# Loading every second weight chunk with a casting DMA of GpSimd, and making its low part by a negation and an adding DMA

## The chip, the cores and the metric

The kernel runs on one core of one Trainium2 chip. The metric is the time of one execution on the device, in microseconds (us), taken as the median of several runs. The core has five engines, which run apart from each other and wait on semaphores: TensorE (PE, matmuls), VectorE (DVE), ScalarE (ACT), GpSimd (POOL) and SyncE (SP). SP and POOL issue DMAs, and all of these run on the core's 16 DMA engines.

## The reference, cut to what matters

A trunk of two layers works on 256 tokens of 1024 features, in float32. Each layer is a feed-forward block, a token mixer and a second feed-forward block, and each of these is wrapped in norms:

```python
x = x + 0.5 * rms_norm(swiglu(rms_norm(x, pre1), w_gate_up1, w_down1), post1)
x = x + rms_norm(hybrid_mixer(rms_norm(x, pre_m), w_in, ..., w_o), post_m)
x = x + 0.5 * rms_norm(swiglu(rms_norm(x, pre2), w_gate_up2, w_down2), post2)
# swiglu(h): g, u = split(h @ w_gate_up); (silu(g) * u) @ w_down,  D_FF = 2816
# hybrid_mixer: z = h @ w_in (6144 columns), a gated width-3 convolution, pooling over
# 2, 4, 8, 16 tokens with small group products, two gated projections, then @ w_o
```

The weights are 216 MB in float32. Every weight is read once.

## The kernel before, in words

**Precision.** A matmul in the type float32r uses only the upper part of a float32's mantissa. To get a float32 product the kernel splits every operand into a high part (`hi`, the value rounded to float32r) and a low part (`lo`, value minus high part). A product is then high times high, high times low, and low times high, summed in PSUM.

**Stream of weights.** The weights are cut into 206 chunks of 128 partitions by 2048 float32 (1.05 MB), listed in the order of use in `stream`. A stage is one sublayer: 33 chunks of a feed-forward block (22 of gate and up by turns, 11 of the down product), or 37 of a mixer. The stages begin at chunks 0, 33, 70, 103, 136 and 173. `issue` (L105) starts a chunk: two DMAs of SP, of 512 KB each, into buffers named `raw` (five halves in all), then four parts for each chunk: ACT casts a half of `raw` into `hi`, DVE subtracts it from `raw` into `lo`, and the same for the second half. The parts are put in the list `parts` and taken from it one by one by `part()`, which stands at chosen places between the other work of ACT and DVE. PE, ACT and DVE keep the order of the program (`InOrder`), while the order on POOL and SP is that of a scheduler.

**Depth.** There are five `hi` and five `lo` buffers (`LOOK + 1`). When the product of chunk i is written, chunk i+4 is started, into the buffers that chunk i-1 leaves. A `raw` buffer is free as soon as DVE has subtracted, so that a DMA into it can run ahead of that.

**Products.** `feat_product` (features on partitions) makes 32 matmuls of one chunk; for each eighth of the chunk a matmul with `hi` is followed by one with `lo`, so both parts are needed at once. `out_product` ends a stage: its last three chunks (`TAIL`) are first used for tokens 0 to 127 (block 0), half of the columns after the other, and then for block 1, the first of the three chunks ahead of the other two. While block 1 is on PE, the norms of block 0 run on ACT, DVE and POOL, and its normed rows are turned by PE and cast into `xt` by ACT (`turn`). `fill` then begins the next stage with its first three chunks, block 0 ahead of block 1, so that block 1's norms are covered in turn. POOL computes the power -0.5 of each norm (tile `r`, L207).

**Evictions.** `add_up` copies one half of a product out of PSUM by ACT and adds the other by DVE. PSUM has eight banks, and a product of features holds two.

Of the kernel before, what the change touches and what calls it, by code (L numbers as in the profile page):

```python
# [10 lines left out]
F32 = mybir.dt.float32  # L11
# [3 lines left out]
ALU = mybir.AluOpType  # L15

P = 128
T = 256
D = 1024
# [16 lines left out]

# Columns of the per-feature parameters: gate bias, conv taps, pool bias, pool scale.
F_BG, F_CW, F_PB, F_PS, F_N = 0, 16, 40, 48, 56


class InOrder:
    """An engine whose instructions are kept in the order of the program."""

# [9 lines left out]
def trunk(ctx: ExitStack, tc: tile.TileContext, x, gains, feat, wgu1, wd1, win, wco, wpg, wpo, wo, wgu2, wd2, out):  # L53
    nc = tc.nc
# [17 lines left out]

# [1 line left out]
    xs = [const.tile([P, D], F32, name=f"x{b}") for b in range(NB)]  # L74
# [12 lines left out]

# [1 line left out]
    stream = []  # L89
# [15 lines left out]
    ready = {}  # L105
    state = {"issued": 0, "used": 0}

    def issue(now=True):
        """Loads and splits the next chunk, or leaves the parts of the split for part()."""
        i = state["issued"]  # L110
        state["issued"] = i + 1
        name, l, c = stream[i]
        hi = whi.tile([P, CHUNK], F32R, name="hi")
        lo = wlo.tile([P, CHUNK], F32R, name="lo")
        h = CHUNK // 2
        for s in range(2):
            sl = slice(s * h, (s + 1) * h)
            raw = raws.tile([P, h], F32, name="raw")
            nc.sync.dma_start(raw, src[name][l, c, :, sl])
            parts.append(lambda sl=sl, raw=raw: act.copy(hi[:, sl], raw))  # L120
            parts.append(
                lambda sl=sl, raw=raw: dve.tensor_tensor(lo[:, sl], raw, hi[:, sl].bitcast(F32), op=ALU.subtract)
            )
        ready[i] = (hi, lo)
        if now:
            part(4)
# [8 lines left out]
    def chunk(name, held=0):  # L135
        """The next chunk; held: how many of the chunks before it are still to be read."""
        i = state["used"]
        assert stream[i][0] == name, (stream[i], name)
        state["used"] = i + 1
        top_up(held + 1)  # L140
        if state["issued"] == i + 1:
            part(len(parts))
        return ready.pop(i)

    def top_up(held):
        """Loads and splits ahead, into the buffers that are not held; held chunks are still to be
        read. The last split is left to part()."""
        part(len(parts))
        while state["issued"] < min(state["used"] + LOOK + 1 - held, len(stream)):
            part(len(parts))  # L150
            issue(False)

# [1 line left out]
    def split(dst, src_ap, between=0):  # L154
        """dst = (high, low) views; src in PSUM or SBUF, float32."""
        hi, lo = dst
        act.copy(hi, src_ap)
        part(between)
        dve.tensor_tensor(lo, src_ap, hi.bitcast(F32), op=ALU.subtract)

    def feat_product(name, acts_hl):
        """W^T @ act for the two 128-column tiles of a chunk, features on partitions. In each of the
        two banks: the high weights with the high and with the low part of act side by side, and the
        low weights with the high part on top of the first."""
        ps = [bank(), bank()]
        whi_, wlo_ = (t.rearrange("p (k c) -> p k c", c=CC) for t in chunk(name))
        for i in range(2):
            cs = slice(i * P, (i + 1) * P)
            for k in range(KT):
                both, ah, _ = acts_hl[k]  # L170
                pe.matmul(ps[i], whi_[:, k, cs], both, start=(k == 0), stop=False)
                pe.matmul(ps[i][:, :T], wlo_[:, k, cs], ah, start=False, stop=(k == KT - 1))
        return ps

    def add_up(ps, tag, out=None):
        """The two halves of a feature product, added: [128, 2, 256]."""
        t = tmp.tile([P, 2, T], F32, name=tag)
        out = t if out is None else out
        for i in range(2):
            act.copy(t[:, i, :], ps[i][:, T:])  # L180
        part()
        for i in range(2):
            dve.tensor_tensor(out[:, i, :], ps[i][:, :T], t[:, i, :], op=ALU.add)
        return out

    def token_product(o, w, acts_hl, b, ks):
        """o[128 tokens of block b, 256] = act^T @ W chunk."""
        whi_, wlo_ = (t.rearrange("p (k c) -> p k c", c=CC) for t in w)
        for n, (i, w) in enumerate(((0, whi_), (1, whi_), (0, wlo_))):
            for k in ks:  # L190
                a = acts_hl[k][1 + i][:, b, :]
                pe.matmul(o, a, w[:, k, :], start=(n == 0 and k == 0), stop=(n == 2 and k == KT - 1))

# [1 line left out]
    def load_gain(l, which):  # L195
# [4 lines left out]
    def rstd(parts, scale):  # L200
        """(scale * (sum of parts / D + eps)) ** -0.5"""
        v0 = small.tile([P, 1], F32, name="v0")
        dve.tensor_scalar(v0, parts[0], scale / D, scale * EPS, op0=ALU.mult, op1=ALU.add)
        v1 = small.tile([P, 1], F32, name="v1")
        dve.tensor_scalar(v1, parts[1], scale / D, v0, op0=ALU.mult, op1=ALU.add)
        r = small.tile([P, 1], F32, name="r")
        nc.gpsimd.tensor_tensor(r, v1, mhalf, op=ALU.pow)  # L207
        return r
# [7 lines left out]
    def post(b, banks, gain, scale):  # L216
        """x[b] += rms(h) * gain / sqrt(scale)"""
        u = wide.tile([P, D], F32, name="u")
# [15 lines left out]
    def pre(b, gain, r=None):  # L234
        """rms(x[b]) * gain"""
        if r is None:
# [8 lines left out]
    def turn(b, s):  # L245
        """Half of the next sublayer's input of block b, features on partitions, split."""
        xn, xt = state["xn"][b], state["next"][0]
# [11 lines left out]
    def act_slot(dtype=F32):  # L259
        """[128, 2, 512] float32, or twice that in bfloat16"""  # L260
        return acts.tile([P, 2, 512], dtype, name="act", tag="act")

    def split_pair(src_ap):
        """Two feature tiles [128, 2, 256] -> (high and low side by side, high, low) of each"""
        t = act_slot(F32R).rearrange("p i (h t) -> p i h t", h=2)
        split((t[:, :, 0, :], t[:, :, 1, :]), src_ap, 1)
        return [(t[:, i], t[:, i, 0, :], t[:, i, 1, :]) for i in range(2)]

# [1 line left out]
    def out_product(name, nchunk, acts_hl, on_block):  # L270
# [40 lines left out]
    def fill(name, n, turns, acts_hl, take):  # L311
        """n chunks' products, tokens on partitions. Block 0 goes ahead, and after turns[s] halves of
        a product the s-th half of block 1's input is turned. take(b, f, ps) reads the columns of
        one or two chunks, the f-th the last."""
        ws = [chunk(name, LOOK) for _ in range(n)]
# [16 lines left out]

# [1 line left out]
    def turn_back(tok):  # L334
        """[128 tokens, 2, 256 features] of both blocks, as [128 features, 2, 256 tokens] in PSUM."""
        pt = bank()
# [5 lines left out]
    def ffn(l, gu, dn, acts_hl, on_block, nfill, turns, gains_):  # L342
        # The first nfill chunks: gate and up of a pair by turns, and a last gate.
        slot = act_slot()
# [31 lines left out]
    def mixer(l, acts_hl, on_block, nfill, turns, gains_):  # L376
# [3 lines left out]

        # Gates of the conv branch, the first of block 0 ahead of block 1.
        slots = [act_slot() for _ in range(2)]
# [22 lines left out]

        # Gated short convolution.
        ys = []
# [17 lines left out]

        # Pooling over trailing windows.
        ds_ = []
# [21 lines left out]

        # Gates of the pool branch.  # L450
        gp = gates()
# [30 lines left out]

# [1 line left out]
    plan = []  # L484
    for l in range(DEPTH):
        plan += [("ffn", l, "gu1", "d1", 0, 1, 4.0), ("mix", l, None, None, 2, 3, 1.0), ("ffn", l, "gu2", "d2", 4, 5, 4.0)]

    # The tensor engine's clock rises only after some time of work.
    idle = act_slot(BF16)[:, 0, :]
# [54 lines left out]
def _cols(w):  # L544
    """[L, 1024, N] -> [L, N / 256, 128, 8 * 256]: chunks of 256 columns, partitions first."""
    l, k, n = w.shape
# [4 lines left out]
def _rows(w):  # L551
    """[L, K, 1024] -> [L, K / 256, 128, 2 * 1024]: chunks of two row tiles, partitions first."""
    l, k, n = w.shape
# [4 lines left out]
def _gate_up(w):  # L558
    """Chunks of gate columns and of up columns by turns."""
    c = _cols(w)  # L560
# [35 lines left out]
```

## Time and profile before

| What | Value |
|---|---|
| median of 3 runs | 1187.08 us (1185.7 to 1188.16) |
| span of the profiled execution, first to last instruction | 1184.7 us |
| median less this span | 2.4 us |
| PE, DVE, ACT busy | 1169.6, 804.2, 639.1 us |
| granted TensorE clock, mean | 0.995 of full speed |
| DMA | 224.48 MB on SP's queue, 190 GB/s over the span |

The profiled execution's own time is not given apart from its span; the span is one execution's, and the three runs lie 1.0 to 3.5 us above it. A busy share counts the time in which an engine has an instruction in work; the busy share of DMA is that of the packets on the 16 DMA engines.

### The profile page before, as it was taken

The page shows a single profiled execution, that of the slowest core. Times are in us where ns is not written, and L with a number is a line of the kernel's source. Part 1 is how long each engine was busy: PE and PEld are TensorE (multiplying, and loading weights), DVE is VectorE, ACT ScalarE, POOL GpSimd, SP SyncE. Part 2 cuts the span into 40 slices and gives each one's busy share as a digit, 9 for nine tenths or more (in the row PEclk, how much of TensorE's full clock was granted, in tenths as well). Part 3 has the DMA queues.
Part 4 walks back from the last instruction along what each step waited for, and adds up shares of the span by engine and source line. Part 5 has one row for each costly group of instructions (what it writes and reads, how often), then busy time and mean ns, then how long its engine had stood idle before and what let it go on. Part 6 is the DMA issues. An engine that isn't in the chain of part 4 may idle for free.

```text
span 1184.7 us, 17127 instructions
## 1 busy us (share of the span) xinstructions
PE 1169.6 (99%) x6625; PEld 1023.1 (86%) x6625; DVE 804.2 (68%) x1092; ACT 639.1 (54%) x997; POOL 17.2 (1%) x75
## 2 busy tenths in 40 slices
PE   7999999999999999999999999999999999999997
PEld 6888888988888898888898888898888888988886
DVE  5776745677987776665476666466789786766742
ACT  5755634655564565554365555356556565655630
POOL 0000000000000000000000000000000000000000
PEclk8999999999999999999999999999999999999999
DMA  7765663655566465667456566536565554756540
GB/s 267 265 188 192 194 228 132 222 184 179 171 202 209 163 230 183 196 190 231 161 193 192 185 195 230 189 128 215 182 204 185 198 181 141 243 184 194 190 167 36
DMA packets 62577, 225.57 MB, mean 190 GB/s; under 512 B 7200, under 2 KB 7200, under 8 KB 62496
## 3 DMA queue, kind: packets, MB, share of 16 engines
q1 hardware_dynamic: 62496, 224.48, 57.5%
q8 instruction: 52, 0.85, 0.3%
q14 instruction: 29, 0.24, 0.1%
HBM read 223.40 MB, written 1.05 MB: 189 GB/s over the span
## 4 chain that ended last, share of the span: by engine, by line
PE 96%; ACT 1%; DVE 1%; DMA 1%; POOL 0%; issue 0%; SPq 0%; DVEq 0%; POOLq 0%; ACTq 0%
PE ps L49 96%; ACT junk L49 1%; DMA x<-in_x 1%; POOL r L207 0%; DVE x L49 0%; DVE xn L49 0%; DVE v L49 0%; DVE lo L49 0%; ACT xt L49 0%; ACT hi L49 0%; SPq L78 0%; DVEq L592 0%; POOLq L592 0%; SPq L197 0%; ACTq L49 0%
## 5 line engine op out<-in xcount | busy, mean ns | idle before, releaser
L49 PE MATMUL ps<-xt,hi 128*128 128x512 f32 x1920 | 667.3, 392 | 0.0
L49 DVE TENSOR_TENSOR lo<-raw,hi 128x1024 fp32r<-128x1024 f32 x412 | 495.0, 1221 | 134.5 <-ACT hi L49 133.5
L49 PE MATMUL ps<-xt,lo 128*128 128x256 f32 x1920 | 537.7, 280 | 0.0
L49 ACT CAST hi<-raw 128x1024 fp32r<-128x1024 f32 x412 | 424.9, 1050 | 103.1 <-PE ps L49 89.1
L49 PEld LDWEIGHTS ps<-xt,hi 128*128 128x128 f32 x1920 | 359.2, 187 | 78.7
L49 PEld LDWEIGHTS ps<-xt,lo 128*128 128x128 f32 x1920 | 362.9, 189 | 0.1
L49 PE MATMUL ps<-hi,act 128*128 128x512 f32 x832 | 260.0, 390 | 0.0
L49 PEld LDWEIGHTS ps<-hi,act 128*128 128x128 f32 x832 | 156.2, 188 | 32.3
L49 PE MATMUL ps<-lo,act 128*128 128x512 f32 x416 | 161.9, 389 | 0.0
L49 ACT COPY h<-ps 128x256 f32<-128x256 f32 x150 | 54.5, 374 | 142.9 <-PE ps L49 141.6
L49 DVE TENSOR_TENSOR h<-ps,h 128x256 f32<-128x256 f32 x150 | 61.6, 420 | 91.7 <-ACT h L49 91.7
L49 ACT COPY sil<-ps 128x256 f32<-128x256 f32 (+1 forms) x126 | 46.7, 374 | 103.5 <-PE ps L49 103.5
L49 PE MATMUL ps<-act,hi 128*128 128x512 f32 (+1 forms) x320 | 102.0, 375 | 0.0
L49 PEld LDWEIGHTS ps<-lo,act 128*128 128x128 f32 x416 | 78.1, 188 | 15.7
L49 PE MATMUL ps<-act,lo 128*128 128x256 f32 x288 | 81.0, 281 | 0.0
L49 DVE TENSOR_TENSOR sil<-ps,sil 128x256 f32<-128x256 f32 x106 | 43.7, 420 | 49.1 <-ACT sil L49 49.1
L49 PE MATMUL ps<-hi,xt 128*128 128x256 f32 x512 | 74.4, 289 | 0.8 <-ACT hi L49 0.8
L49 ACT CAST act<-h 128x512 fp32r<-128x512 f32 x65 | 40.4, 621 | 60.9 <-DVE h L49 60.9
L49 PEld LDWEIGHTS ps<-hi,xt 128*128 128x128 f32 x512 | 67.7, 196 | 1.6 <-ACT hi L49 1.2
L49 PEld LDWEIGHTS ps<-act,hi 128*128 128x128 f32 x320 | 58.1, 189 | 12.0
L49 PEld LDWEIGHTS ps<-act,lo 128*128 128x128 f32 x288 | 54.5, 189 | 0.0
L49 DVE TENSOR_TENSOR act<-h,act 128x512 fp32r<-128x512 f32 (+1 forms) x73 | 50.1, 686 | 6.0 <-ACT act L49 5.7
(57 smaller groups left out, 450.2 us busy)
## 6 DMA issues: line engine op xcount, KB each, us to landing
raw<-in_wgu SPq DMA_DIRECT2D x176, 512.0 KB, 4.6
raw<-in_win SPq DMA_DIRECT2D x96, 512.0 KB, 4.7
raw<-in_wd SPq DMA_DIRECT2D x88, 512.0 KB, 4.6
raw<-in_wco SPq DMA_DIRECT2D x16, 512.0 KB, 5.2
raw<-in_wpo SPq DMA_DIRECT2D x16, 512.0 KB, 4.2
raw<-in_wo SPq DMA_DIRECT2D x16, 512.0 KB, 4.4
gain<-in_gains SPq DMA_DIRECT2D x12, 512.0 KB, 4.6
raw<-in_wpg SPq DMA_DIRECT2D x4, 512.0 KB, 4.2
```

What stands on the lines that cost most here:

```text
L49: return lambda *a, **kw: self.tc.keep_in_program_order(f(*a, **kw))
```

## The change: what it does

From chunk 5 on, every odd chunk (5, 7, ... 205: 101 of the 206) takes another way. One DMA of POOL of 1.05 MB reads the weights from HBM and casts them into `hi`. ACT writes `lo = -hi`, in two halves. A second DMA of POOL reads the same weights again and adds them onto `lo`, which leaves value minus high part. These chunks use no `raw` buffer and nothing of DVE. The list of parts has for such a chunk the two negations, the issue of the adding DMA, and an empty part, so that the places of `part()` stay in step. The even chunks, and chunks 1 and 3, stay as they were. The comments were taken out, too, which moves the line numbers.

```diff
         hi = whi.tile([P, CHUNK], F32R, name="hi")
         lo = wlo.tile([P, CHUNK], F32R, name="lo")
         h = CHUNK // 2
+        ready[i] = (hi, lo)
+        if i > 3 and i % 2:
+
+            w = src[name][l, c]
+            nc.gpsimd.dma_start(hi, w)
+            for s in range(2):
+                sl = slice(s * h, (s + 1) * h)
+                parts.append(lambda sl=sl: act.mul(lo[:, sl], hi[:, sl].bitcast(F32), -1.0))
+            parts.append(lambda: nc.gpsimd.dma_start(lo, w, accum_op=ALU.add))
+            parts.append(lambda: None)
+            if now:
+                part(4)
+            return
         for s in range(2):
...
-        ready[i] = (hi, lo)
         if now:
             part(4)
```

On ACT, in the first gate and up stage, before the change. Here `ps_716` and `ps_717` are the banks of an up product, `hi_721` is chunk 13, four further on than that product's, and `sil_812` takes the next gate product:

```order
L49 COPY h_759<-ps_716 128x256 [waits PE_49,Activation_49]
L49 COPY h_759<-ps_717 128x256 [waits PE_49]
L49 CAST hi_721<-raw_723 128x1024 [waits DMAHW2_49]
L49 CAST act_766<-h_759 128x2x256 [waits DVE_49]
L49 CAST hi_721<-raw_725 128x1024 [waits DMAHW3_49]
L49 COPY sil_812<-ps_770 128x256 [waits PE_49,Activation_49]
L49 COPY sil_812<-ps_771 128x256 [waits PE_49]
```

The same place after the change; `ps_700` and `ps_701` are the same product, and chunk `hi_705`, `lo_706` is the same chunk, number 13:

```order
L49 COPY h_740<-ps_700 128x256 [waits PE_49,Activation_49]
L49 COPY h_740<-ps_701 128x256 [waits PE_49]
L49 ACTIVATE lo_706<-hi_705 128x1024 [waits DMASW0_49]
L49 CAST act_747<-h_740 128x2x256 [waits DVE_49]
L49 ACTIVATE lo_706<-hi_705 128x1024
L49 COPY sil_792<-ps_751 128x256 [waits PE_49,Activation_49]
L49 COPY sil_792<-ps_752 128x256 [waits PE_49]
```

The two casts, which waited for SP's DMA into `raw`, are now two negations, and the first of them waits for POOL's DMA into `hi` (DMASW), at the same place between the evictions.

On ACT at the end of the first stage, before the change. `x0_88` is block 0 of x; `ps_1773` and `ps_1794` are its turned halves; `hi_1780` is chunk 35, the third chunk of the next stage; `ps_1394` and `ps_1395` are block 1's sums:

```order
L49 ACTIVATE junk_1734,ss_1735<-x0_88 128x512 [waits DVE_49,Activation_49]
L49 ACTIVATE junk_1737,ss_1738<-x0_88 128x512 [waits DVE_49,Activation_49]
L49 CAST xt_1716<-ps_1773 128x512 [waits PE_49]
L49 CAST hi_1780<-raw_1782 128x1024 [waits DMAHW6_49]
L49 CAST xt_1716<-ps_1794 128x512 [waits PE_49]
L49 ACTIVATE junk_1808,ss_1809<-ps_1394 128x512 [waits Activation_49]
L49 ACTIVATE junk_1812,ss_1813<-ps_1395 128x512 [waits PE_49,Activation_49]
L49 CAST hi_1780<-raw_1784 128x1024 [waits DMAHW7_49]
```

The same place after the change, where chunk 35 is `hi_1720`, `lo_1721`:

```order
L49 ACTIVATE junk_1674,ss_1675<-x0_88 128x512 [waits DVE_49,Activation_49]
L49 ACTIVATE junk_1677,ss_1678<-x0_88 128x512 [waits DVE_49,Activation_49]
L49 CAST xt_1656<-ps_1713 128x512 [waits PE_49]
L49 ACTIVATE lo_1721<-hi_1720 128x1024 [waits DMASW6_49,DMASW5_49]
L49 ACTIVATE lo_1721<-hi_1720 128x1024
L49 CAST xt_1656<-ps_1731 128x512 [waits PE_49]
L49 ACTIVATE junk_1745,ss_1746<-ps_1351 128x512 [waits Activation_49]
L49 ACTIVATE junk_1749,ss_1750<-ps_1352 128x512 [waits PE_49,Activation_49]
```

Both negations of chunk 35 now stand between the two casts of `xt`, and behind the wait for its DMA.

On POOL at the same place, before the change; `r_1729` and `r_1744` are the powers for block 0's two norms, `r_1820` and `r_1836` those for block 1:

```order
L207 TENSOR_TENSOR r_1729<-v1_1727,mhalf_95 128x1 [waits DVE_49]
L207 TENSOR_TENSOR r_1744<-v1_1742,mhalf_95 128x1 [waits DVE_49]
L207 TENSOR_TENSOR r_1820<-v1_1818,mhalf_95 128x1 [waits DVE_49,Pool_49]
L207 TENSOR_TENSOR r_1836<-v1_1834,mhalf_95 128x1 [waits DVE_49,Pool_49]
```

After the change, where `r_1669` and `r_1684` are block 0's and `r_1757` and `r_1772` block 1's, and `lo_1581` and `lo_1721` are chunks 33 and 35:

```order
L120 DMA hi_1580<-in_win 128x2048 [waits DMASW4_49,DVE_49,PE_49]
L124 DMA lo_1581<-in_win 128x2048 [waits DMASW5_49,Activation_49]
L219 TENSOR_TENSOR r_1669<-v1_1667,mhalf_95 128x1 [waits DVE_49]
L120 DMA hi_1720<-in_win 128x2048 [waits DMASW6_49,PE_49]
L219 TENSOR_TENSOR r_1684<-v1_1682,mhalf_95 128x1 [waits DVE_49]
L124 DMA lo_1721<-in_win 128x2048 [waits DMASW7_49,Activation_49]
L219 TENSOR_TENSOR r_1757<-v1_1755,mhalf_95 128x1 [waits DVE_49,Pool_49]
L219 TENSOR_TENSOR r_1772<-v1_1770,mhalf_95 128x1 [waits DVE_49,Pool_49]
```

The load of chunk 35 into `hi`, which waits for PE to leave the buffer, now stands ahead of the second power of block 0, and its adding DMA, which waits for ACT's negations, ahead of both powers of block 1.

## Rows read from the trace of the kernel before

**Rows 1.** The page's busy times: engine, busy us, share of the span, instructions.

```profile
span 1184.7 us, 17127 instructions
...
PE 1169.6 (99%) x6625; PEld 1023.1 (86%) x6625; DVE 804.2 (68%) x1092; ACT 639.1 (54%) x997; POOL 17.2 (1%) x75
```

**Rows 2.** The page's DMA part: packets, MB, share of the 16 engines; then HBM traffic.

```profile
q1 hardware_dynamic: 62496, 224.48, 57.5%
...
HBM read 223.40 MB, written 1.05 MB: 189 GB/s over the span
```

**Rows 3.** The page's chain that ended last, by engine: shares of the span.

```profile
PE 96%; ACT 1%; DVE 1%; DMA 1%; POOL 0%; issue 0%; SPq 0%; DVEq 0%; POOLq 0%; ACTq 0%
```

**Rows 4.** Groups of instructions: line engine op, shapes, count, busy us, mean ns, idle before.

```profile
L49 DVE TENSOR_TENSOR lo<-raw,hi 128x1024 fp32r<-128x1024 f32 x412 | 495.0, 1221 | 134.5 <-ACT hi L49 133.5
...
L49 ACT CAST hi<-raw 128x1024 fp32r<-128x1024 f32 x412 | 424.9, 1050 | 103.1 <-PE ps L49 89.1
```

**Rows 5.** All waits: who waited for whom, us in total, times, longest us.

```profile
ACT hi L49 <- DMA raw<-in_wgu: 8.1, 18, 1.6
```

**Rows 6.** Tile raw: time of an issue on SP (ns min/median/max), us to landing.

```profile
L119 SPq DMA_DIRECT2D raw<-in_wgu x176: 327/328/1705, 3.1 to 1087.7; - x176
...
DMA to landing us min/median/max: 3.5/4.6/10.3
```

**Rows 7.** DMA from 1150 us to the end, when only the output is stored.

```profile
q1 hardware_dynamic: 576, 1.05, 8.1%
```

**Rows 8.** Busy us by engine in a stretch, granted clock, DMA share, GB/s.

```profile
1010.00:1020.00 10.00, 10.00 (x67) 9.04 (x66) 8.12 (x9) 7.49 (x11) 0.00 (x0) 1.00 0.94 343
```

**Rows 9.** Timeline of ACT in a gate and up stage: start, us, instruction, idle before.

```profile
73.19 0.37 ACT L49 COPY h<-ps 128x256 f32<-128x256 f32 x1 [2.35 <-PE ps L49]
...
84.28 0.37 ACT L49 COPY h<-ps 128x256 f32<-128x256 f32 x1 [2.35 <-PE ps L49]
```

**Rows 10.** Timeline of ACT at the end of the first feed-forward stage.

```profile
177.87 2.01 ACT L49 CAST hi<-raw 128x1024 fp32r<-128x1024 f32 x2 [3.43 <-PE ps L49]
183.31 2.01 ACT L49 CAST hi<-raw 128x1024 fp32r<-128x1024 f32 x2 [3.43 <-PE ps L49]
187.38 0.60 ACT L49 ACTIVATE junk<-ps 128x512 bf16<-128x512 f32 x1 [2.07 <-PE ps L49]
...
191.53 0.60 ACT L49 ACTIVATE junk<-ps 128x512 bf16<-128x512 f32 x1 [3.45 <-PE ps L49]
...
197.92 0.59 ACT L49 CAST xt<-ps 128x512 fp32r<-128x512 f32 x1 [2.47 <-PE ps L49]
...
199.76 0.59 ACT L49 CAST xt<-ps 128x512 fp32r<-128x512 f32 x1 [0.30 <-PE ps L49]
200.25 0.60 ACT L49 ACTIVATE junk<-ps 128x512 bf16<-128x512 f32 x1
...
210.65 0.59 ACT L49 CAST xt<-ps 128x512 fp32r<-128x512 f32 x1 [1.29 <-PE ps L49]
```

**Rows 11.** Timeline of PE at the same place.

```profile
197.25 0.63 PE L49 MATMUL ps<-ident,xn 128*128 128x128 f32 x4 [0.39 <-DVE xn L49]
...
207.66 0.64 PE L49 MATMUL ps<-lo,xt 128*128 128x256 f32 x4
208.14 0.60 PE L49 MATMUL ps<-ident,xn 128*128 128x128 f32 x4
...
219.08 0.40 PE L49 MATMUL ps<-xt,hi 128*128 128x512 f32 x1
```

**Rows 12.** Busy us by engine in two stretches of the same place, DMA share, GB/s.

```profile
192.00:196.00 4.00, 4.00 (x19) 3.33 (x18) 2.60 (x6) 1.66 (x6) 0.77 (x2) 1.00 0.02 6
196.00:200.00 4.00, 3.61 (x20) 2.77 (x19) 2.62 (x4) 1.78 (x3) 0.32 (x1) 1.00 0.00 0
```

**Rows 13.** Timeline of POOL at the same place.

```profile
192.54 0.55 POOL L207 TENSOR_TENSOR r<-v,mhalf 128x1 f32<-128x1 f32 x1 [180.35 <-DVE v L49]
195.77 0.55 POOL L207 TENSOR_TENSOR r<-v,mhalf 128x1 f32<-128x1 f32 x1 [2.69 <-DVE v L49]
```

## The prediction

> **What bounds the kernel now.** I read the page's busy times first. PE is busy for 1169.6 of 1184.7 us; all of its idle time is 15.1 us, while DVE and ACT have a third and more to spare [rows 1]. The chain that ended last lies on PE for 96% [rows 3]. So nothing that makes DVE or ACT faster can give back more than a part of 15.1 us, and the question is whether the new way of the odd chunks still delivers in time. Two views say how much room there is. The DMA engines are busy for 57.5% of the span with 224.48 MB [rows 2], which is 681 us of all 16 together, or 3.18 us for a chunk of 1.05 MB. And ACT, which casts the loaded weights, waited only 8.1 us in all for loads of gate and up weights, 1.6 us at the longest [rows 5]: loads are hidden, because a raw buffer is free long before hi is.
>
> In a gate and up stage ACT's copies of the same kind are 84.28 - 73.19 = 11.09 us apart for two chunks, 5.55 us each [rows 9]. In the down product a chunk takes 183.31 - 177.87 = 5.44 us [rows 10].
>
> **What it removes.** 202 of 412 subtractions of DVE at 1.221 us, 247 us, and 202 casts of ACT at 1.050 us, in whose place 202 negations of the same size come [rows 4]; I price these at 1.05 us too, since ACT's row is the nearest. 202 loads of SP go, whose issues took 0.33 us each [rows 6]. DVE, ACT and SP are not what PE waits for, so all of this is worth nothing on the path; PE's work is the same, instruction by instruction.
>
> **What it adds: traffic.** Each of 101 chunks is read twice, and its second DMA also reads lo in SBUF. No row shows a casting or an adding DMA. The casting one moves the bytes of a plain load, and I price it as one, 3.18 us of the 16 engines. For the adding one the lower end is a plain load again, 3.18 us: the read of SBUF would lie wholly beside that of HBM. The nearest row for a read of SBUF is the final store: 1.05 MB took 8.1% of 34.7 us, 2.81 us [rows 7]. If an engine reads its two sources one after the other, an adding DMA costs 3.18 + 2.81 = 5.99 us. I take this value: a load's 16 engines are held for the time of the read, and here there are two reads to one write. Above that no row gives an end; three passes, 9 us, I use as one.
>
> The DMA engines then have 681 + 101 x 5.99 = 1286 us of work, 101 us more than the whole span; at the lower end 681 + 321 = 1002 us, 85% of it. They decide as soon as an adding DMA costs more than (1185 - 21 - 681) / 101 = 4.8 us; the 21 us are the end, below.
>
> The Trainium skill (Collectives: The Full Stack, the part on why ReduceScatter is half of AllGather) says that a reducing transfer of DMA is slowed not by its addition but by its two source reads, which share one read ring, and gives a measured ratio of 1.93. That is a collective between cores and no run here shows it; taken over as twice a load it would make 681 + 101 x 6.36 = 1323 us, an estimate, against 1286 by the rows.
>
> **What it adds: a chain.** The hi buffer of chunk i is free when PE ends chunk i-5, and lo is wanted when PE begins chunk i. Between lie the casting load, the negations, and the adding DMA. A load of 512 KB lands 4.6 us after its issue in the median, 3.5 at least [rows 6]; the other half adds 1.6 us of engine time, so I put the casting load at 6.2 us (5.1 to 8). The negations are 2 x 1.05 us with ACT's cast of 0.6 us between them, 2.7 us. The adding DMA lands after 6.2 us at the low price and 9.0 at the middle one. In all 15.1 or 17.9 us, where no other transfer shares the engines; writing the descriptors on POOL has no row, and SP's 0.33 us is the nearest one, so I add nothing and hold 1 to 2 us a DMA as the upper bound. Four chunks between are 22.2 us, so inside a stage the chain fits and its delay is hidden by four chunks of PE.
>
> ACT is in order, so a negation that waits holds the evictions behind it. Its place is after the copies of the next product but three, some 6 us after the buffer is free, about when the load lands; ACT has 2.35 us of idle time there [rows 9] and PSUM holds four products. That costs nothing.
>
> At the ends of stages the room is smaller. From ACT's sums, half of a block takes 191.53 - 187.38 = 4.15 us, so a chunk's step in one half takes 0.69 us and block 0 begins at 183.2 [rows 10]. The third of the last three chunks is wanted after four such steps: 2 x 5.44 + 2.8 = 13.7 us after its buffer came free. It is odd in three stages (69, 135, 205). The chain is late there by 1.4 us at the low price, 4.2 at the middle one. The third chunk of the next stage gets the buffer of the first of the last three, free at 191.5 + 2.8 = 194.3; its lo is wanted at 207.66 [rows 11], 13.4 us on. It is odd at three stage starts (35, 105, 175): late by 1.7 or 4.5 us. And its negations wait for a load that lands at 200.5, ahead of the cast of xt that stood at 199.76 and of block 1's sums [rows 10]; they end at 202.6, some 2.8 us late, and PE needs that half of xt. In raw's place the cast there was ready at once. On POOL the load's wait for PE stands ahead of block 0's second power, which ran at 195.77 [rows 13]; the buffer is free before that, so it is hidden. The chunk after the filling ones (73, 139) has its negations behind the cast of 210.65 [rows 10], so at 213.3, and lands at 219.5 against 219.08 [rows 11]: 0.4 us, or 3.2. The sum is 3 x 1.4 + 3 x 4.5 + 2 x 0.4 = 18 us at the low price, 3 x 4.2 + 3 x 7.3 + 2 x 3.2 = 41 at the middle one.
>
> **The sum.** At the middle price the DMA engines are the bound, and I do not add the 41 us: they are idle time of PE in which the backlog of transfers runs. What is added is the end. After the last chunk's lo has landed, 20 of 24 steps are left, 13.8 us, and I give half of PE's 15.1 us of idle time to what follows the last matmul, so 21 us. The span becomes 1286 + 21 = 1307 us; the median of the runs lies 2.4 us above the span, so **1310 us**.
>
> **The rivals.**
>
> *The adding DMA costs a plain load.* Then the engines have 15% to spare, PE stays the bound, and only the 18 us at the stage ends count: 1205 us, up to 1230 with descriptors at 1 to 2 us. For it: DMA shows 0.94 busy at 343 GB/s in one stretch [rows 8], against 189 at 57.5% [rows 2], so a busy share overstates the engines' need by a tenth. Against it: the second read has to go somewhere.
>
> *The adding DMA costs three passes or more*, because each row is read, added and written before the next: 681 + 909 + 21 + 2 = 1613 us. No row speaks for it or against it.
>
> *No change*: the chain is shorter than I think at the stage ends, as DMA is idle there (0.02 and 0.00 busy from 192 to 200 us [rows 12]) and loads land in the 3.5 us minimum. With 1.1 us off each DMA the chain is 12.9 us, under all the rooms above, and only the cast of xt is behind by 1.7 us, which block 0's first half covers: 1187 us.
>
> *Faster*: the stage ends lose their waits. On the chain block 1's norms and sums lie behind casts and subtractions of ACT and DVE; DVE now has less in front of the rows of xn. PE waits 0.39 us for these at a stage end [rows 11], five times 0.39 is 2 us; it decides only where the odd chunks are never late, so 1185 us, hardly outside of what a measurement can tell.
>
> **How the numbers follow.** Middle price 0.50, plain load 0.30, three passes 0.10, no change 0.06, faster 0.04. The time is that of the first. Its own range is 1240 to 1390: if the engines work at 343 / 0.94 = 365 GB/s throughout and not at 330, their 1286 us become 1161 and the stage ends alone decide, with 41 us and a shared DMA's delay, 1240; if the 8 us of idle time of DMA at each of five stage ends remain, 1350, and with shared engines' longer landings some 40 more. The whole range, 1190 to 1400, takes in the plain load and leaves out three passes, faster and no change, 0.20. A measurement of this kernel tells about 0.2%, 2.4 us, from no change: faster 0.04, same 0.06, slower 0.90.
>
> **What would show it.** Right: PE's busy share falls to about 90%, with waits of PE for lo, released by POOL's DMAs, throughout the stages and not only at their ends; the DMA share is above 0.9 in all slices; DVE's busy time is about 557 us, ACT's about the same as now; an adding DMA lands 9 us or more after its issue. The plain load is right if the DMA share stays near 85% and PE's waits stand at the stage ends alone. The prediction is wrong if PE's waits are for ACT, behind a negation, or if the landing of the casting loads, not of the adding ones, is what lengthens.

## Result and the profile after

The changed kernel takes 1571.89 us in the median of three runs (1571.11 to 1572.73), against 1187.08 us before: 1.3246 times as long (95% interval 1.3228 to 1.3263), 385 us more. The sign was forecast, the size was not: 1310 us, with 1190 to 1400 as the range.

The page of the kernel after, its lines on busy times (as [rows 1]), DMA queues (as [rows 2]; q0 is POOL's queue, q1 SP's), the chain (as [rows 3]), groups of instructions (as [rows 4]) and issues of DMAs with their median time to landing:

```profile
span 1570.1 us, 16905 instructions
...
PE 1282.5 (82%) x6625; PEld 1088.0 (69%) x6625; DVE 567.6 (36%) x890; ACT 620.8 (40%) x997; POOL 161.4 (10%) x277
...
q0 software_dynamic: 29088, 211.83, 54.0%
q1 hardware_dynamic: 33408, 118.56, 20.0%
...
issue 72%; DMA 10%; POOL 8%; PE 6%; ACT 3%; DVE 2%; POOLq 0%; SPq 0%; DVEq 0%; ACTq 0%
...
L49 PE MATMUL ps<-xt,lo 128*128 128x256 f32 x1920 | 565.7, 295 | 123.6 <-DMA lo<-in_wgu 88.3
L49 ACT ACTIVATE lo<-hi 128x1024 fp32r<-128x1024 f32 x202 | 208.7, 1054 | 782.0 <-DMA hi<-in_wgu 298.6
...
hi<-in_wgu POOLq DMA_DIRECT2D x42, 1024.0 KB, 11.6
lo<-in_wgu POOLq DMA_DIRECT2D x42, 1024.0 KB, 8.4
```

Two things are to be seen. No engine is full: PE is idle for 288 us, ACT and DVE have less to do than before, and the DMA queues together (54.0 and 20.0%, and 0.2% for loading instructions) hold the 16 engines for 74.2%, 1165 us of the span, which is less than the whole time of before. And the casting load into `hi`, which moves 1.05 MB, lands only 11.6 us after its issue, later than the adding DMA. A kernel in which nothing is full and everything waits has a loop: something that comes back to itself by way of waits. The table of waits says by way of whom (waiter, released by whom, us in total, times, longest):

```profile
POOL lo L124 <- ACT lo L49: 424.6, 36, 17.8
...
ACT lo L49 <- DMA hi<-in_wgu: 298.6, 35, 11.6
...
PE ps L49 <- DMA lo<-in_wgu: 95.1, 37, 4.9
...
POOL hi L120 <- PE ps L49: 49.9, 10, 10.0
```

POOL, about to issue the adding DMA, waits for ACT's negation; ACT's negation waits for the load into `hi`; and that load is issued by POOL. Only ten times did the load itself wait for PE. (The adding DMA's waits stand in two more rows, by the names of ACT's neighbouring copies; the timelines tell which instruction ended them.) The timeline of POOL in the first gate and up stage (start, us, instruction, idle time before it):

```profile
113.12 0.86 POOL L124 DMA_DIRECT2D lo<-in_wgu  x1 [13.56 <-ACT sil L49]
113.68 0.87 POOL L120 DMA_DIRECT2D hi<-in_wgu  x1
128.13 0.86 POOL L124 DMA_DIRECT2D lo<-in_wgu  x1 [13.59 <-ACT sil L49]
128.69 0.87 POOL L120 DMA_DIRECT2D hi<-in_wgu  x1
```

And ACT in the same cycle, where the second negation ends at 127.84:

```profile
115.67 0.66 ACT L49 COPY h<-ps 128x256 f32<-128x256 f32 x2
125.31 1.06 ACT L49 ACTIVATE lo<-hi 128x1024 fp32r<-128x1024 f32 x1 [8.98 <-DMA hi<-in_wgu]
126.27 0.60 ACT L49 CAST act<-h 128x512 fp32r<-128x512 f32 x1
126.78 1.06 ACT L49 ACTIVATE lo<-hi 128x1024 fp32r<-128x1024 f32 x1
```

The cycle can be added up. The adding DMA of one odd chunk is issued at 113.12. The casting load of the next odd chunk stands right behind it on POOL and on its queue: issued at 113.68 (0.56 us later), landed at 125.31 (11.63 us). The two negations with a cast between them end at 127.84 (2.53 us), and the next adding DMA is issued at 128.13 (0.29 us). That is 15.0 us for two chunks, where PE needs 11.09 [rows 9]. All issues of adding DMAs, in the view of line L124 (count, issue time in ns, first and last start):

```profile
L124 POOL DMA_DIRECT2D lo<-in_wgu x42: 841/857/892, 35.9 to 1453.3; - x42
...
L124 POOL DMA_DIRECT2D lo<-in_wd x22: 841/854/892, 174.2 to 1537.3; - x22
```

From the first at 35.9 us to the last at 1537.3, 100 cycles take 1501.4 us, 15.01 us each. So the loop is not the state of one stage. It is not even, though: 56 of the 100 cycles lie within 0.5 us of 15.0, and the others run from 3.8 to 23.0 us, the longest about the ends of stages.

In this stage PE waits once in a cycle, here until 121.56 us, 8.4 us after the issue at 113.12, which is when that add lands:

```profile
121.56 0.55 PE L49 MATMUL ps<-xt,lo 128*128 128x256 f32 x1 [3.67 <-DMA lo<-in_wgu]
137.57 0.35 PE L49 MATMUL ps<-xt,lo 128*128 128x256 f32 x1 [2.13 <-DMA lo<-in_wgu]
```

### The profile page after: what moved, and what is told of

It reads as the page before. It is cut to its first block, busy times and chain, and to the rows that moved or that the text cites. A ratio compares the mean times of both kernels' runs of the same rounds, so it can differ in the third digit from the quotient of the medians.

```text
span 1570.1 us, 16905 instructions
## 1 busy us (share of the span) xinstructions
PE 1282.5 (82%) x6625; PEld 1088.0 (69%) x6625; DVE 567.6 (36%) x890; ACT 620.8 (40%) x997; POOL 161.4 (10%) x277
## 3 DMA queue, kind: packets, MB, share of 16 engines
q1 hardware_dynamic: 33408, 118.56, 20.0%
HBM read 329.31 MB, written 1.05 MB: 210 GB/s over the span
## 4 chain that ended last, share of the span: by engine, by line
issue 72%; DMA 10%; POOL 8%; PE 6%; ACT 3%; DVE 2%; POOLq 0%; SPq 0%; DVEq 0%; ACTq 0%
PE ps L49 6%; DMA hi<-in_win 4%; POOL hi L120 4%; POOL lo L124 3%; DMA lo<-in_wd 2%; DMA lo<-in_wo 1%; ACT lo L49 1%; DMA hi<-in_wgu 1%; DMA hi<-in_wd 1%; DVE h L49 1%; ACT junk L49 0%; POOL r L219 0%; DMA x<-in_x 0%; DVE lo L49 0%; ACT hi L49 0%
## 5 line engine op out<-in xcount | busy, mean ns | idle before, releaser
L49 PE MATMUL ps<-xt,hi 128*128 128x512 f32 x1920 | 720.7, 415 | 8.4 <-ACT act L49 7.3
L49 PE MATMUL ps<-xt,lo 128*128 128x256 f32 x1920 | 565.7, 295 | 123.6 <-DMA lo<-in_wgu 88.3
L49 ACT ACTIVATE lo<-hi 128x1024 fp32r<-128x1024 f32 x202 | 208.7, 1054 | 782.0 <-DMA hi<-in_wgu 298.6
L49 PEld LDWEIGHTS ps<-xt,lo 128*128 128x128 f32 x1920 | 386.8, 201 | 138.9 <-issue 120.0
L49 PEld LDWEIGHTS ps<-xt,hi 128*128 128x128 f32 x1920 | 384.8, 200 | 99.8 <-ACT act L49 7.9
L49 DVE TENSOR_TENSOR lo<-raw,hi 128x1024 fp32r<-128x1024 f32 x210 | 252.6, 1221 | 285.9 <-ACT hi L49 285.6
L49 PE MATMUL ps<-hi,act 128*128 128x512 f32 x832 | 279.6, 416 | 1.5 <-ACT act L49 1.5
L49 ACT CAST hi<-raw 128x1024 fp32r<-128x1024 f32 x210 | 215.9, 1049 | 5.3 <-DMA raw<-in_wgu 5.3
L124 POOL DMA_DIRECT2D lo<-in_wgu x42 | 36.1, 858 | 531.5 <-ACT sil L49 192.8
L49 PE MATMUL ps<-lo,xt 128*128 128x256 f32 x256 | 43.2, 293 | 9.6 <-DMA lo<-in_wgu 6.8
## 6 DMA issues: line engine op xcount, KB each, us to landing
hi<-in_wgu POOLq DMA_DIRECT2D x42, 1024.0 KB, 11.6
```

Of the source, the lines that this page charges most:

```text
L49: return lambda *a, **kw: self.tc.keep_in_program_order(f(*a, **kw))
L124: parts.append(lambda: nc.gpsimd.dma_start(lo, w, accum_op=ALU.add))
```

## The experiments

Three theories. **L**, the loop: add, the next casting load behind it on POOL's queue, negations, next add. **D**, the forecast: the time of the DMA engines. **A**: the negation that waits on ACT holds the evictions behind it, and PE stands for want of PSUM. Later two theories on what remained are added. The kernel before was run beside each set, at 1186.08 to 1187.97 us.

### e1: the odd chunks loaded by SP

```diff
-            nc.gpsimd.dma_start(hi, w)
             for s in range(2):
+                raw = raws.tile([P, h], F32, name="raw")
+                nc.sync.dma_start(raw, w[:, sl])
+                parts.append(lambda sl=sl, raw=raw: act.copy(hi[:, sl], raw))
                 parts.append(lambda sl=sl: act.mul(lo[:, sl], hi[:, sl].bitcast(F32), -1.0))
-            parts.append(lambda: nc.gpsimd.dma_start(lo, w, accum_op=ALU.add))
-            parts.append(lambda: None)
+            last = parts.pop()
+            parts.append(lambda: (last(), nc.gpsimd.dma_start(lo, w, accum_op=ALU.add)))
```

> Odd chunks are loaded into raw by SP and cast into hi by ACT as before, and lo is made by ACT's negation and POOL's adding DMA; the bytes and the 101 adding DMAs are those of the changed kernel. Theory L (the loop): the changed kernel's 15.0 us for two chunks is a cycle on POOL's queue, adding DMA, then the next casting load behind it (lands 11.6 us later), then negations (2.5 us), then the next adding DMA; with the load off that queue the cycle is gone, and PE is the bound again: 1190 to 1230 us. Theory D (the DMA engines' time decides, as I predicted): nothing is taken off the engines, 1500 us or more. Theory A (a negation that waits holds ACT's evictions): also 1190 to 1230, since nothing waits long.

Measured: 1308.18 us, 1.1014 (1.0982 to 1.1046). That is 264 us less than the changed kernel with the same bytes read and the same adds, so D is out as the cause of 1572. It is 121 us more than before, above the 1190 to 1230 of L. POOL's timeline shows the loop gone inside the stage, and the windows (busy us of PE, PEld, DVE, ACT and POOL, then clock, DMA share, GB/s) show PE busy throughout, at DMA engines that are full:

```profile
116.88 0.88 POOL L127 DMA_DIRECT2D lo<-in_wgu  x1 [10.22 <-ACT sil L49]
127.97 0.88 POOL L127 DMA_DIRECT2D lo<-in_wgu  x1 [10.22 <-ACT sil L49]
```

```profile
110.00:120.00 10.00, 10.00 (x59) 8.82 (x58) 4.34 (x8) 8.23 (x12) 0.88 (x1) 1.00 1.00 295
```

The page of this kernel gives the price of an adding DMA by itself, as POOL's queue holds nothing else:

```profile
q1 hardware_dynamic: 62496, 224.48, 46.4%
q0 software_dynamic: 14544, 105.91, 42.8%
```

42.8% of 1306.7 us for 101 adds is 5.54 us each (by the same working 5.69 in e8 and 5.61 in e10). e1 changes more than the queue: the odd chunks' loads now go into `raw`, so that they no longer wait for a free `hi`. What the two are worth apart has no run.

### e2: the next casting load ahead of the add

```diff
-            nc.gpsimd.dma_start(hi, w)
+            pool.dma_start(hi, w)
+            while adds:
+                adds.pop(min(adds))()
...
-            parts.append(lambda: nc.gpsimd.dma_start(lo, w, accum_op=ALU.add))
+            parts.append(lambda: adds.update({i: lambda: pool.dma_start(lo, w, accum_op=ALU.add)}))
...
+        if i in adds:
+            adds.pop(i)()
         return ready.pop(i)
```

> On POOL the casting load of the next odd chunk is put ahead of the adding DMA of the one before; nothing else is changed. Theory L: the cycle is cut; the adding DMA now stands behind a load that waits for its buffer, and lands some 12.5 us after it, where 11.1 us are free, so 12.5 us for two chunks and about 1300 us (1250 to 1370). Theory D: the same bytes, within 3% of 1572. Theory A: the negations still wait for their loads, at most by some us less: 1450 to 1570.

Measured: 1452.14 us, 1.2226 (1.2077 to 1.2375). Inside the stage the two DMAs have changed places, and the cycle is 12.5 us:

```profile
108.02 0.55 POOL L49 DMA_DIRECT2D hi<-in_wgu  x1 [9.73 <-PE ps L49]
108.56 0.91 POOL L49 DMA_DIRECT2D lo<-in_wgu  x1
120.54 0.55 POOL L49 DMA_DIRECT2D hi<-in_wgu  x1 [11.07 <-PE ps L49]
121.08 0.91 POOL L49 DMA_DIRECT2D lo<-in_wgu  x1
```

The load now lands after 6.9 us and the add after 12.3 us (medians of the page), against 11.6 and 8.4 in the changed kernel: whichever is second in the queue pays 4 to 5 us. 120 us come back, and D falls again. But L's range was missed by 80 us, and the total lies in A's (1450 to 1570), so by itself this run does not decide between L and A. POOL's timeline shows where L's total was short: the casting loads are 12.57 us apart in the median, as expected, and 13.96 on average, which makes 139 us in 100 cycles. 125 of these 139 stand in the 37 cycles that begin within seven chunks of one of the five changes of stage. About one of these changes POOL sits 20.50 us, until 722 us, before the power of a norm with the next load behind it, and then 18.85 us, until 760 us, before a load whose buffer PE has not left.

### e3: every fourth chunk instead of every second

```diff
-        if i > 3 and i % 2:
+        if i > 3 and i % 4 == 1:
```

> Only every fourth chunk (5, 9, 13, ...) takes the new way, 51 of 206. Theory L: one cycle of 15.0 us for four chunks, of which PE needs 22.2 us, so nothing is left inside of the stages: 1190 to 1220. Theories D and A as a price for each chunk of the new way: half of the loss, about 1380 (1340 to 1420).

Measured: 1215.78 us, 1.0236 (1.0135 to 1.0337; its two runs lie 10 us apart). As L says: a loop of at most 15 us fits into the 22.2 us of four chunks. A price for each chunk of the new way, by ACT or by the DMA engines, would have left about half of the loss. D in the form of the prediction, engines with more work than time, is not tested here: with 51 adds it forecasts no loss either (e8's expectation has the sum); e1 and e11 are what speaks against it. What is left lies, by PE's timeline, at the ends of stages and in the first chunks of the next: seven waits for a `lo` of 0.9 us or more, 15.7 us together, the longest 4.42 us at a mixer's last product.

On POOL the casting load is issued 11.87 us after the last add, so that this add has landed (8.2 us) and nothing of POOL's queue is ahead of the load:

```profile
77.42 0.86 POOL L124 DMA_DIRECT2D lo<-in_wgu  x1 [9.75 <-ACT sil L49]
89.29 0.56 POOL L120 DMA_DIRECT2D hi<-in_wgu  x1 [11.01 <-PE ps L49]
100.19 0.85 POOL L124 DMA_DIRECT2D lo<-in_wgu  x1 [10.34 <-ACT sil L49]
```

```profile
hi<-in_wgu POOLq DMA_DIRECT2D x21, 1024.0 KB, 8.0
```

From the load's issue to the landing of its own add are 10.90 + 8.2 = 19.1 us, less than four chunks of PE.

### e4: the negations on POOL

```diff
-                parts.append(lambda sl=sl: act.mul(lo[:, sl], hi[:, sl].bitcast(F32), -1.0))
+                parts.append(lambda sl=sl: nc.gpsimd.tensor_scalar(lo[:, sl], hi[:, sl].bitcast(F32), -1.0, None, op0=ALU.mult))
```

> The negations are made by POOL and not by ACT, so that neither ACT nor DVE ever waits for a casting load. Theory A: the evictions are free again, below 1300. Theory L: POOL itself waits in the cycle, which keeps its parts; a negation of 128x1024 on POOL has no row, at 1 to 2 us each the cycle is 14.5 to 17 us: 1500 to 1780. Theory D: the bytes are the same, within 3% of 1572.

Measured: 1792.04 us, 1.5088 (1.5044 to 1.5132). A falls: no negation stands on ACT any more, and it is slower still. By L the loop has grown by the slower negations; the timeline of POOL shows one turn of it, 16.68 us from add to add, in which two negations take 5.51 us (1.06 us each on ACT):

```profile
104.02 0.89 POOL L124 DMA_DIRECT2D lo<-in_wgu  x1 [0.30 <-DVE h L49]
104.62 0.86 POOL L120 DMA_DIRECT2D hi<-in_wgu  x1
114.90 5.51 POOL L123 TENSOR_SCALAR lo<-hi 128x1024 fp32r<-128x1024 f32 x2 [9.41 <-DMA hi<-in_wgu]
120.70 0.90 POOL L124 DMA_DIRECT2D lo<-in_wgu  x1 [0.30 <-POOL lo L123]
```

Over the run the adds are 17.21 us apart on average, and the total is 12 us above L's range. As the loop grows in the same run, e4 shows that A is not the main cause, not that waits on ACT cost nothing; e6 shows more.

### e5 and e6: the second DMA left out, or a plain load in its place

```diff
-            parts.append(lambda: nc.gpsimd.dma_start(lo, w, accum_op=ALU.add))
+            parts.append(lambda: None)
```

> The changed kernel without its adding DMAs, so that lo of an odd chunk is left at minus hi; the casting loads and the negations stay. Theory L: nothing stands ahead of the casting load, which lands in 6.5 to 7.5 us and not in 11.6; the cycle is 10 to 11 us, under PE's 11.1 for two chunks: 1187 to 1215. Theory C (GpSimd's casting load is itself slow): it lands later than 9 us still, and the time stays above 1300.

Measured: 1194.35 us, 1.0083 (1.0061 to 1.0104), as L says. The casting load, the negations and POOL's issues together cost 0.8% (0.6 to 1.0).

```diff
-            parts.append(lambda: nc.gpsimd.dma_start(lo, w, accum_op=ALU.add))
+            parts.append(lambda: nc.gpsimd.dma_start(lo, w))
```

> The second DMA of an odd chunk is a plain casting load of the weights into lo, which adds nothing (lo is then the whole weight); its place and its waits are the same. It measures what the adding costs on the queue. If an adding DMA holds the engines 5.5 us and a load about 2.9, the casting load behind it lands 2.6 us earlier, the cycle is 12.4 us, and the time some 1310 (1280 to 1350). If the addition costs the engines nothing, the cycle stays 15.0 us and the time is within 3% of 1572.

Measured: 1242.55 us, 1.0473 (1.0362 to 1.0584), below the expected 1280 to 1350: the load behind a plain one lands after 7.8 us, not 9.0, and the loop is 11.1 us, as long as PE's two chunks. Issues of the two kernels, e5 first:

```profile
hi<-in_wgu POOLq DMA_DIRECT2D x42, 1024.0 KB, 5.2
```

```profile
hi<-in_wgu POOLq DMA_DIRECT2D x42, 1024.0 KB, 7.8
lo<-in_wgu POOLq DMA_DIRECT2D x42, 1024.0 KB, 5.2
```

So the landing of the casting load is 5.2 us with nothing ahead of it, 7.8 behind a plain load, 11.6 behind an add. These are the loop's one long part in three lengths; with the last, the time goes from 1242.55 to 1571.89 us. Of e6's 56 us over before, most stand at the ends of stages: its adds are 11.19 us apart in the median, and of the 52 us that 100 cycles lie above this, 46 are in the 37 cycles about the ends, counted as in e2.

e6 also speaks against A. Its negations wait for their loads on ACT for 435.0 us in all, 5.15 us in a cycle of the first gate and up stage, and PE's timeline has no wait there from 100 to 125 us. In the changed kernel itself PE waited 254.2 us for the adding DMAs, of 288 us of idle time in all:

```profile
L49 ACT ACTIVATE lo<-hi 128x1024 fp32r<-128x1024 f32 x202 | 208.8, 1054 | 435.0 <-DMA hi<-in_wgu 175.0
```

### e7: SP's loads, and no add

e1 with the adding DMA left out (`parts.append(last)`).

> The kernel with SP's loads for all chunks (1308 us) without its adding DMAs; lo of an odd chunk is left at minus hi. ACT does the same 202 casts and 202 negations more than the changed kernel's. If that kernel's remaining loss is the DMA engines' (1.00 busy in its stages, so that a stage end is not made up for), 1187 to 1195 us. If it is ACT's added work, above 1220.

Measured: 1185.46 us, 0.9995 (0.9981 to 1.0009). ACT's 202 further operations (1199 against 997; the expectation counts the 202 negations as well, which the changed kernel has already) cost nothing; e1's 121 us come with the adds.

### e8: SP's loads, every fourth chunk

e1 with e3's condition. It asks whether e1's 121 us come from full DMA engines.

> SP's loads for all chunks, and the negation and adding DMA for every fourth chunk alone (51). With 5.5 us of engine time for each adding DMA the DMA engines have 606 + 51 x 5.5 = 887 us of work, 75% of the span of before. If saturation is what is left at 1308 us, 1187 to 1205; if each adding DMA has its price at PE wherever it stands, half of that loss, about 1248.

Measured: 1247.14 us, 1.0512 (1.0471 to 1.0552). Half of the adds make half of the loss, while the DMA engines' share has gone from e1's 89.2% to 74.5% (both queues), so saturation over the whole run falls as its cause. It looks like a price for each add, but PE's waits for a `lo` are few and long: eight of 2 us or more, 39 us together, all in the first chunks of a stage or among a mixer's last products. The largest, on PE's timeline, is at the mixer's last product, for an add that POOL issued at 411.32:

```profile
411.32 0.86 POOL L127 DMA_DIRECT2D lo<-in_wo  x1 [23.24 <-ACT lo L49]
```

```profile
421.67 0.77 PE L49 MATMUL ps<-lo,act 128*128 128x512 f32 x1 [8.21 <-DMA lo<-in_wo]
```

ACT's timeline there has four operations for this chunk (cast, negation, cast, negation) among its evictions and other casts, and the add follows the last:

```profile
405.37 1.05 ACT L49 CAST hi<-raw 128x1024 fp32r<-128x1024 f32 x1
407.42 0.62 ACT L49 CAST act<-h 128x512 fp32r<-128x512 f32 x1 [0.99 <-DVE h L49]
407.94 1.06 ACT L49 ACTIVATE lo<-hi 128x1024 fp32r<-128x1024 f32 x1
408.91 1.03 ACT L49 CAST hi<-raw 128x1024 fp32r<-128x1024 f32 x1
409.97 1.06 ACT L49 ACTIVATE lo<-hi 128x1024 fp32r<-128x1024 f32 x1
```

While this add is under way, SP's loads for the next stage run beside it, and the DMA engines are 0.96 busy (415 to 420 us). So full engines over the run are not the cause, but for single adds at the ends of stages they are not excluded.

### e9, e10 and e11: the new way inside the stages alone

The last question: does each add have its price wherever it stands, or is what remains in e1 and e8 lost at the ends of stages and in the mixer's last products, where buffers come free later against the use of the next chunk?

```diff
+    MID = [i for b, n in ((0, 30), (33, 24), (70, 30), (103, 30), (136, 24), (173, 30)) for i in range(b + 8, b + n)]
...
-        if i > 3 and i % 2:
+        if i in MID and i % 2:
```

e9 is e8 with this list (and `i % 4 == 1`), e10 is e1 with it, and e11 is the changed kernel with it.

> As the run with every fourth chunk by SP's load, cast, negation and POOL's adding DMA, but only where the chunk and the five before it lie inside a stage: from the ninth chunk of each stage on, without the last three of a feed-forward stage and without the last thirteen of a mixer (30 chunks instead of 51). If the 60 us of that run are lost at the ends of stages and in the mixer's last products: 1187 to 1195 us, with no wait of PE for a lo over 2 us. If each adding DMA has its price wherever it stands (60 / 51 = 1.2 us): 1187 + 30 x 1.2 = 1222.

Measured: 1189.55 us, 1.0025 (1.0014 to 1.0036), 3 us over before, with no wait of PE for a `lo` over 2 us.

> The same places, every odd chunk there (60 of the 101), by SP's load, cast, negation and POOL's adding DMA. If the remaining 121 us of the run with all odd chunks by SP are lost at the ends of stages: 1187 to 1215, since a cycle of two chunks measured 11.1 to 11.3 us inside the stages there, against 11.09 before. If each adding DMA has its price wherever it stands: 1187 + 60 x 1.2 = 1259.

Measured: 1203.24 us, 1.0129 (1.0096 to 1.0163). The group of PE's products with `lo` in e9, then in e10: of idle time before them, 1.2 and 7.4 us are left.

```profile
L49 PE MATMUL ps<-xt,lo 128*128 128x256 f32 x1920 | 537.4, 280 | 1.2 <-DMA lo<-in_wgu 1.0 <-ACT sil L49 0.2
```

```profile
L49 PE MATMUL ps<-xt,lo 128*128 128x256 f32 x1920 | 539.7, 281 | 7.4 <-ACT act L49 3.4 <-DMA lo<-in_win 2.6 <-DMA lo<-in_wgu 0.7
```

Both as expected of a loss at the ends; a price for each add would have given 1222 and 1259. So of e1's 121 us, the 60 chunks inside the stages make 15 (1.29% of 1186) and the other 41, put beside them, some 105. POOL's timeline of e1 agrees: its adds are 11.31 us apart in the median, and the 37 cycles about the ends of stages hold 120 us above that, the other 63 on balance none.

> The changed kernel's own way (casting load and adding DMA on POOL's queue), for the same 60 odd chunks inside the stages alone. Theory L, the loop of casting load, negations, adding DMA and next casting load on POOL's queue of 15.0 us: 60 x (15.0 - 11.09) = 234, less some 4 us of room at the begin of each of six stretches: 1187 + 234 - 24 = 1397 (1370 to 1430). The rival that the change's loss, too, is made at the ends of stages: 1187 to 1215, as for the run by SP's loads.

Measured: 1376.96 us, 1.1615 (1.1595 to 1.1636), in L's range. At the very chunks at which SP's loads lose 15 us, POOL's queue loses 191, or 3.2 us for an odd chunk. The two ways of loading differ in the queue and in the buffer that SP's load goes into, not in the adds; and inside these stretches the changed way keeps L's loop, with adds 14.94 us apart in the median.

## Why the prediction was wrong

**What bounds the kernel now** was right: PE, with all else hidden. **What it removes** was right too: DVE came out at 567.6 us (557 forecast), ACT at 620.8, and e7 shows that the work on ACT and DVE is worth nothing either way.

**What it adds: traffic** was nearly right in its price and wrong as a bound. An adding DMA was put at 5.99 us of engine time, two reads in series, and takes 5.54 (e1), against 2.92 to 3.15 for one of the same queue that only casts (e6: 47.8% of 1235.5 us for 202; e5: 26.7% of 1191.7 us for 101). The ratio is 1.76 to 1.90. The Trainium skill's 1.93 for a reducing transfer of a collective (Collectives: The Full Stack, the part on why ReduceScatter is half of AllGather) is a little above that; whether two source reads are the reason here too, no run shows. But 1286 us of work became 1165 (314 on SP's queue, 848 on POOL's, 3 elsewhere); the adds' price makes 45 of these 121 us, and the rest is that the plain loads, too, held the engines for less than their 3.18 us a chunk of before (2.78 us on SP's queue: 314 us for 118.56 MB). And 1165 lies below the 1184.7 us of the span before: the engines were never the bound of this kernel. In e1, inside the stage shown, they were full, and PE did not wait. That e1 came out at 1308 us, almost the forecast, is chance: in e10 the engines are as full there (a share of 1.00 from 110 to 120 us), and 105 of e1's 121 us are gone.

**What it adds: a chain** is the step that failed. The prediction added up the chain of one odd chunk, 17.9 us, compared it with four chunks of PE, 22.2 us, and wrote: "So inside a stage the chain fits and its delay is hidden by four chunks of PE." As a latency this holds where the chain stands alone: 19.1 us in e3. But the next odd chunk comes after 11.09 us, not 22.2, so two such chains overlap, and they share POOL and its queue, in which the next chunk's casting load is issued behind the adding DMA of the one before and lands behind it. The add can't be issued before its negations, and these wait for the load of the same chunk, which waited for the add before. What had to be compared with 11.09 us was not the chain's length but the part of it that one chunk hands to the next: issue 0.56, landing of the load behind the add 11.63, negations 2.53, issue 0.29, in all 15.0. From these (15.0 - 11.09) x 101 = 395 us follow; 385 were measured. The order of instructions showed it ahead of the run: in POOL's order after the change, the `lo` DMA of chunk 33 stands ahead of the `hi` DMA of chunk 35.

**The casting load** was put at 6.2 us. It is 5.2 by itself (e5), and 11.6 where it stands. The prediction named this as one sign of its being wrong, the landing of the casting loads lengthening and not that of the adding ones; so it was: the adds, put at 9.0 us, land after 8.4. The Trainium skill (DMA: Bandwidth & Descriptors, on two DMAs through the same engine) says that in one queue of one DMA engine descriptors start in order, though pipelined. That agrees with 5.2, 7.8 and 11.6 us, and with e2, where the two DMAs changed places and the landings with them. It is not all of it: in e3 the load has nothing ahead of it in the queue and still lands after 8.0 us, not 5.2. There SP's loads land later as well, after 6.5 us against 4.8 in e5; so a part of the 11.6 us is likely what other transfers take from the same engines, which no run has parted from the order.

**The wait on ACT** is not the cost, but the reason given for that was wrong: it is 8.98 us in a cycle, far more than the 2.35 us of ACT's idle time that were to cover it. It is a link of the loop: e4, without it on ACT, gains nothing, and in e6 435.0 us of such waits leave PE without a wait inside the stage shown.

**The ends of stages** do lose time where the loop is away: 105 us in e1, which loads by SP, against the 41 us that the prediction had for the changed kernel. There they are covered by the loop, which keeps to 15.01 us on average over all of the run: the 37 cycles about the ends hold only 16 us above the median, against 120 in e1. Why an add costs more at the ends of e1 and e8 is read from one place of e8 only: the add is issued late, behind ACT's other work, and PE goes on 10.35 us after that issue (adds of gate and up land after 11.0 us in e8's median, beside SP's loads, and 8.2 in e3's). How the 105 us divide between the late issue and the slow landing was not separated.

The changed kernel's PE is also busy for 113 us more, at a mean clock of 0.923. By the loop that is a consequence: the casting load waited for PE only ten times, 49.9 us in all, so a faster PE would mostly have waited longer for the same landings. No run tried it.

No kernel of these beats the one before. DVE, ACT and SP, which the change relieves, are not what PE waits for.

## What to carry to other kernels

For a chain of steps that is started again for every second chunk, add up two things: its length, to be compared with the depth of the buffers, and the turn from one chunk's step to the same step of the next by way of shared queues, to be compared with the pace; each alone can set the time. Where a DMA that waits for an engine stands in one queue with the load that feeds that engine, look at what stands behind it, and keep the load on another queue if it can be (here that took a cast by ACT and a buffer). When every engine has room in the profile, look for a period in the issues of one line, and add up one turn of it from the timelines.

## What the hardware showed that was not expected

- The time from issue to landing of the same 1.05 MB casting load on POOL's queue was 5.2, 7.8 or 11.6 us in kernels that issue nothing, a plain load or an adding DMA ahead of it. The add lengthens it by 3.8 us over a plain load, though it holds the engines only 2.4 to 2.6 us longer (5.54 against 2.92 to 3.15). What stands ahead is not all: in e3, with nothing ahead, it was 8.0 us.
- Moving the odd loads from POOL's queue to SP's, into `raw`, took off 264 us (e1), while the 16 engines were held for as long as before the move (89.4% of 1306.7 us, 1168 us, against 1165). The Trainium skill (DMA: Bandwidth & Descriptors, rules for kernel authors) says that spreading DMAs over the issuing engines doesn't help bandwidth; the trace agrees, and what was gained are waits.
- POOL needs 2.81 us on average (202 of them, e4) for a negation of 128x1024 that ACT does in 1.05.
- After a wait of PE its granted clock can fall. In the cycle after the change (windows with the columns of e1's), PE was idle from 119 to 121 us and ran at 0.50, the 1.2 GHz level, in the next 4 us. The next cycle, 128.13 to 143.00, holds a wait of 2.13 us, and its mean was 1.00.

```profile
113.00:119.00 6.00, 4.88 (x29) 4.03 (x27) 4.56 (x7) 3.32 (x7) 1.42 (x2) 1.00 0.76 131
119.00:121.00 2.00, 0.00 (x0) 0.00 (x0) 0.00 (x0) 0.00 (x0) 0.00 (x0) 0.74 0.94 252
121.00:125.00 4.00, 3.44 (x11) 2.99 (x12) 0.00 (x0) 0.00 (x0) 0.00 (x0) 0.50 1.04 410
...
128.13:143.00 14.87, 12.74 (x74) 10.89 (x73) 4.66 (x8) 4.89 (x9) 1.43 (x2) 1.00 0.79 213
```
